# A hybrid DiT layer: sums of squares by tile pairs, modulation per tile, and the feed-forward's first two blocks by token halves

## The chip, the cores and the metric

One core of a Trainium2 chip runs the whole layer in one launch. The metric is device time in microseconds, from the start to the end of the program; the median of several runs counts. The engines are named as in the profile: PE (TensorE), DVE (VectorE), ACT (ScalarE), POOL (GpSimd) and SP (the queue that issues nearly all transfers).

## The reference, cut to what matters

One layer with 1024 latent tokens and 256 context tokens, width 1024, feed-forward width 2816, everything in fp32:

```python
mod_x = silu(c) @ w_ada + b_ada          # six vectors: sh1, sc1, g1, sh2, sc2, g2
mod_c = silu(c_ctx) @ w_ada + b_ada      # the same map for the context
px = modulate(rms_norm(x, norm1_w), sh1, sc1) @ w_in
pc = modulate(rms_norm(ctx, norm1_w), csh1, csc1) @ w_in
# gated DeltaNet on four heads, neighbourhood attention on eight heads
x = x + g1 * (concat(dn_x, na_x) @ w_out)
x = x + g2 * swiglu(modulate(rms_norm(x, norm2_w), sh2, sc2), w_ffn_in, w_ffn_out)
# modulate(h, shift, scale) = h * (1 + scale) + shift;  swiglu: (silu(gate) * up) @ w_out
```

## The kernel before, in words

The channels lie on the partitions: x is eight tiles `xt[k]` of 128 channels by 1280 tokens (256 context tokens, then 1024 latent ones). An fp32 product is made of three faster ones: each operand is cast to a rounded high part (`hh`, `whi`, `uhi`, `hB`, `hT`) and the rest is its low part (`hl`, `wlo`, `ulo`, `lB`, `lT`); PE adds high by high, high by low and low by high in PSUM. Most of the order is laid out by a list scheduler from the order in the source, and each engine then works strictly in that order; buffers come from pools, and a tile that takes over a place waits for the readers of the one before.

**The head (lines 617 to 715).** SP loads the eight x tiles, the constants, two modulation weight tiles, the raw weights of the first two projection blocks (`fraw`) and six more modulation tiles (`wada`, 1 MB each). ACT squares the tiles, DVE adds seven of them into one tile `acc`. PE multiplies `acc` and the last square by a matrix of ones (line 687), so that every partition holds each token's sum; ACT makes the reciprocal root `rs` from it with Ln and Exp (689, 690), for which it loads function tables. The first modulation (shift and scale) comes in four steps `ada(q)`, each for two channel tiles: 16 products of two `wada` tiles with the silu of both condition vectors, spread over four column groups (662); ACT copies the result to `arow` (665); four small products with a selector `sel` turn it into columns and sum the four groups (668); DVE adds the bias and makes scale times norm weight (`mod1`, `w1s`, lines 671 and 674). `sel` is reduced from the identity matrix by DVE (683). Tile by tile, DVE scales (701), ACT adds the shift and casts to `hh` (702), DVE makes `hl` (704), and PE multiplies the tile into the first two blocks, two key heads (`b.mm([k])`, line 397), six banks of PSUM for 1280 tokens each. The modulation step for the next two tiles stands behind the products of tiles 0, 1 and 2. ACT casts the two blocks' weights and DVE makes their low parts (`prefetch`, 193 and 194). The third block's weights take the buffers of the first block's, so their cast (193) waits for its last product.

**The middle.** The other projection blocks, the chunked scans in two directions, the attention, and the output projection, which the change does not touch.

**The feed-forward's start (lines 1360 to 1530).** The output projection ends with the residual stream `x2` in two halves of 512 tokens. For each half `normed(t)` sums the squares on PE (1373) and makes `rs`; `quadrant("Bij")` scales, shifts and splits four channel tiles (i: channel half, j: token half; 1461, 1462, 1454, 1455). B12 lies in the tiles that the profile calls `hT` and `lT`, which later hold the sum T4. The first two of 22 feed-forward blocks (`PLAIN`) are made plainly: for each of the blocks f, for each token half t, two products of 24 matmuls over the channel halves (1279), then Silu and a product on DVE. The order is f 0: first half, second half; f 1: first half, second half. `normed(1)` stands behind the first product. The weight pieces come from `Stream`: `load` fetches them, `make` casts and splits them into one of six buffers each (`uhi`, `ulo`; 1340, 1341), and `ahead(n)` makes them until n are in hand. The remaining 20 blocks go in pairs by a seven-product scheme of Strassen's kind, whose sums of the operand (`sums`, T1 to T4) DVE makes step by step beside the plain blocks. A `Background` called `late` makes the last part of the modulation beside these, with a step behind every second product.

Of the kernel before, what the change touches and what calls it, by code (L numbers as in the profile page):

```python
# [9 lines left out]
F32 = mybir.dt.float32  # L10
# [4 lines left out]
OP = mybir.AluOpType  # L15
# [39 lines left out]
PACE = 0.72  # L55
ORDER = [list(range(NCH)), [1, 0] + list(range(9, 1, -1))]
# [31 lines left out]
def hybrid(ctx, tc, a, dbg):  # L88
# [20 lines left out]
    bias = lasting("bias", [128, 2])  # L109
# [10 lines left out]
    act.dma_start(prm, a["prm"])  # L120
    cst = const("cst", [128, NCONST])
# [61 lines left out]
    def weights(wp, raws=2):  # L183
        def load(src, kt=KT, n=128, lo_engine=pool, raw=None):
# [8 lines left out]
            act.copy(h, r)  # L193
# [175 lines left out]
    with ExitStack() as bs:  # L369
# [30 lines left out]
        class Block:  # L400
# [7 lines left out]
            def prefetch(self, raw=None, lo_engine=pool):  # L408
# [3 lines left out]
                self.w = load_w(src, lo_engine=lo_engine, raw=raw)  # L412
# [207 lines left out]
        with ExitStack() as xs:  # L620
# [15 lines left out]
            sp.dma_start(cst, a["cst"])  # L636
            raws = [xp.tile([128, KT, 128], F32, name=f"fraw{i}", tag=f"fraw{i}") for i in range(2)]
            for j in range(2):
                load_ada(j)
            for i in range(2):  # L640
                sp.dma_start(raws[i], a["w_conv"][4 + i])
            for j in range(2, 8):
                load_ada(j)
            sp.dma_start(cw, a["cw"])
            sp.dma_start(masks, a["masks"])
# [6 lines left out]
            sel = xp.tile([128, 2], F32, name="sel", tag="sel")  # L652
            rs = xp.tile([128, T], F32, name="rs", tag="rs")
            acc = xp.tile([128, T], F32, name="acc", tag="acc")

            def ada(q):

                p = bank("pm")
                for j in (2 * q, 2 * q + 1):
                    w = aw.pop(j)  # L660
                    for k in range(4):
                        pe.matmul(p[32 * k:32 * k + 32], wide[:, 4 * (j % 2) + k], w[:, k], start=j % 2 == 0,
                                  stop=j % 2 == 1)
                row = xp.tile([128, 512], F32, name="arow", tag="arow", bufs=2)
                act.copy(row, p)
                p = bank("pm")
                for b in range(4):
                    pe.matmul(p[:, 2 * b:2 * b + 2], row[:, b * 128:(b + 1) * 128], sel, start=True, stop=True)
                k = slice(2 * q, 2 * q + 2)
                m = mod1.rearrange("p (s b) c -> p s b c", s=2)[:, :, k]  # L670
                dve.tensor_tensor(m, p[:, 0:8].rearrange("p (s b c) -> p s b c", s=2, c=2),
                                  bada[:, 0:16].rearrange("p (s b c) -> p s b c", s=2, c=1)[:, :, k].to_broadcast(
                                      [128, 2, 2, 2]), OP.add)
                dve.scalar_tensor_tensor(w1s[:, k], m[:, 1], 1.0,
                                         n1w[:, k].rearrange("p (b c) -> p b c", c=1).to_broadcast([128, 2, 2]),
                                         op0=OP.add, op1=OP.mult)

            for k in range(KT):
                sq = xp.tile([128, T], F32, name="sq", tag="sq", bufs=2)
                act.activation(sq if k else acc, xt[k], AF.Square)  # L680
                if 0 < k < KT - 1:
                    dve.tensor_tensor(acc, acc, sq, OP.add)
            dve.tensor_reduce(sel, ident.rearrange("p (c i) -> p i c", i=32)[:, 0:2], AX.X, OP.add)
            sums = [bank() for _ in SEGS]
            for i, x in enumerate((acc, sq)):
                for p, (s0, n) in zip(sums, SEGS):
                    pe.matmul(p[:, :n], M[C_ONE], x[:, s0:s0 + n], start=i == 0, stop=i == 1)
            for p, (s0, n) in zip(sums, SEGS):
                act.activation(rs[:, s0:s0 + n], p[:, :n], AF.Ln, bias=b_eps, scale=1.0 / D)
            act.activation(rs, rs, AF.Exp, scale=-0.5)  # L690
            ada(0)
            for b, raw in zip(first, raws):
                b.prefetch(raw, dve)
            for k in range(KT):
                if k == 4:
                    ascope.close()
                    h_tiles(pools(bs, "hp2", "right"), 4)
                t = xt[k]
                parts = [(j, x, mod1[:, k, j:j + 1]) for j, x in ((1, slice(0, CT)), (0, slice(CT, T)))]
                for j, x, sh in parts:  # L700
                    dve.scalar_tensor_tensor(t[:, x], t[:, x], w1s[:, k, j:j + 1], rs[:, x], op0=OP.mult, op1=OP.mult)
                    act.activation(hh[k][:, x], t[:, x], AF.Identity, bias=sh)  # L702
                for j, x, sh in parts:
                    dve.scalar_tensor_tensor(hl[k][:, x], t[:, x], sh, hh[k][:, x].bitcast(F32),
                                             op0=OP.add, op1=OP.subtract)
                for b in first:
                    b.mm([k])
                if k < 3:
                    ada(k + 1)
                if k == 5:  # L710
                    act.copy(mr[:, 4], ident)
                    for d in range(2):
# [990 lines left out]
```

## Time and profile before

| | |
|---|---|
| median of 3 runs | 1579.22 us (1577.59 to 1583.54) |
| the profiled execution's own time | 1576.81 us |
| its span in the trace | 1575.0 us |
| PE busy | 1476.1 us (94%) |
| DVE busy | 997.3 us (63%) |
| ACT busy | 719.8 us (46%) |
| POOL busy | 224.4 us (14%) |
| transfers | 271.02 MB |

Rows of a timeline give the start in us from the span's start, the duration, the engine, the line, the operation, output and inputs, shapes, how many instructions are merged, and in brackets how long the engine stood idle before and who ended it. A PE row counts each fp32 matmul as two instructions. Line numbers in the profile of before are those of the kernel before; from line 56 on the changed kernel's are higher by 1 to 26.

### The profile page before, as it was taken

What the parts mean: (1) busy time and instruction counts of PE and PEld (TensorE: products, weight loads), DVE (VectorE), ACT (ScalarE), POOL (GpSimd) and SP (SyncE); (2) the same over time, 40 slices, a digit from 0 to 9 for tenths busy, and PEclk for the clock granted to TensorE, in tenths of its full rate; (3) what the DMA queues carried; (4) which work ended last, traced back from release to release, by engine and by line L of the source; (5) the groups of instructions that cost most, each with busy time, mean ns of one, the idle gap of its engine ahead of it and who ended that gap; (6) DMA issues with size and microseconds to landing.
All of it is one profiled execution on the core that took longest, in us unless ns stands there. A gap on an engine that the chain in (4) does not pass through costs nothing. (4 is left out here: it accounts for less than half of the span.)

```text
span 1575.0 us, 23911 instructions
## 1 busy us (share of the span) xinstructions
PE 1476.1 (94%) x8626; PEld 1230.5 (78%) x8626; DVE 997.3 (63%) x1846; ACT 719.8 (46%) x1373; POOL 224.4 (14%) x278
## 2 busy tenths in 40 slices
PE   3999999999989887998899999999999999999999
PEld 2788787679887766787688878888888888888887
DVE  4675496674253644678887459865555556689652
ACT  5442553563343544665664256333333333444441
POOL 0045501632353600111100000000000000000000
PEclk8999999999999998999999999999999999999999
DMA  9164221576445449999845711533322224698742
GB/s 388 59 198 140 67 75 65 184 226 215 130 157 189 164 134 295 258 285 283 255 135 188 240 40 59 198 112 113 111 105 101 101 101 135 224 376 291 251 152 83
DMA packets 206406, 271.02 MB, mean 172 GB/s; under 512 B 15952, under 2 KB 115792, under 8 KB 205264
## 3 DMA queue, kind: packets, MB, share of 16 engines
q1 hardware_dynamic: 200816, 264.73, 51.2%
q10 hardware_dynamic: 5472, 4.76, 0.9%
q8 instruction: 68, 1.11, 0.3%
q14 instruction: 50, 0.41, 0.1%
HBM read 204.68 MB, written 68.94 MB: 174 GB/s over the span
## 5 line engine op out<-in xcount | busy, mean ns | idle before, releaser
L397 PE MATMUL blk<-hh,whi 128*128 128x512 f32 (+1 forms) x416 | 125.1, 395 | 4.2 <-ACT hh L702 2.8
L1340 ACT CAST uhi<-ws 128x512 fp32r<-128x512 f32 x91 | 54.8, 623 | 151.5 <-PE ps L1279 77.1
L1340 ACT CAST uhi<-wq 128x512 fp32r<-128x512 f32 x101 | 60.3, 621 | 136.8 <-issue 61.3
L397 PE MATMUL blk<-hh,wlo 128*128 128x512 f32 (+1 forms) x416 | 119.5, 381 | 0.6 <-POOL wlo L194 0.6
L397 PE MATMUL blk<-hl,whi 128*128 128x512 f32 (+1 forms) x416 | 118.9, 379 | 0.0
L1341 DVE TENSOR_TENSOR ulo<-wq,uhi 128x512 fp32r<-128x512 f32 x101 | 67.3, 688 | 65.9 <-ACT uhi L1340 36.5
L1279 PE MATMUL ps<-hT,uhi 128*128 128x512 f32 x336 | 104.3, 392 | 3.1 <-ACT hT L1454 3.1
L1279 PE MATMUL ps<-lT,uhi 128*128 128x512 f32 x336 | 103.6, 390 | 0.0
L1279 PE MATMUL ps<-hT,ulo 128*128 128x512 f32 x336 | 103.4, 389 | 0.0
L1279 PE MATMUL ps<-hB,uhi 128*128 128x512 f32 x288 | 89.7, 392 | 0.0
L1279 PE MATMUL ps<-lB,uhi 128*128 128x512 f32 x288 | 89.2, 391 | 0.0
L1279 PE MATMUL ps<-hB,ulo 128*128 128x512 f32 x288 | 88.8, 389 | 0.0
L397 PEld LDWEIGHTS blk<-hh,whi 128*128 128x128 f32 x416 | 71.0, 194 | 20.8 <-issue 4.9
L397 PEld LDWEIGHTS blk<-hh,wlo 128*128 128x128 f32 x416 | 74.6, 195 | 15.8 <-POOL wlo L194 0.9
L397 PEld LDWEIGHTS blk<-hl,whi 128*128 128x128 f32 x416 | 74.2, 194 | 15.8 <-issue 1.7
L1341 DVE TENSOR_TENSOR ulo<-ws,uhi 128x512 fp32r<-128x512 f32 x91 | 60.9, 687 | 37.6 <-ACT uhi L1340 29.3
L580 PE MATMUL blk<-zhi,hh 128*128 128x256 f32 (+1 forms) x288 | 84.5, 293 | 0.0
L580 PE MATMUL blk<-zhi,hl 128*128 128x256 f32 (+1 forms) x288 | 82.9, 288 | 0.0
L580 PE MATMUL blk<-zlo,hh 128*128 128x256 f32 (+1 forms) x288 | 81.6, 283 | 0.0
L1279 PEld LDWEIGHTS ps<-hT,uhi 128*128 128x128 f32 x336 | 63.1, 189 | 16.5 <-ACT hT L1454 3.5
L194 POOL TENSOR_TENSOR wlo<-wraw,whi 128x1024 fp32r<-128x1024 f32 x18 | 45.0, 2501 | 202.7 <-ACT whi L193 189.1
L1279 PEld LDWEIGHTS ps<-lT,uhi 128*128 128x128 f32 x336 | 63.3, 189 | 13.3
(353 smaller groups left out, 3626.2 us busy)
## 6 DMA issues: line engine op xcount, KB each, us to landing
wq<-w_fo SPq DMA_DIRECT2D x99, 256.0 KB, 5.0
wq<-w_gu SPq DMA_DIRECT2D x88, 256.0 KB, 3.0
wad<-wa SPq DMA_DIRECT2D x64, 256.0 KB, 3.6
bt<-rpb SPq DMA_DIRECT2D x64, 192.0 KB, 4.5
t_d<-g SPq DMA_DIRECT2D x22, 512.0 KB, 4.1
fr<-t_d SPq DMA_DIRECT2D x44, 256.0 KB, 4.6
f_d<-g SPq DMA_DIRECT2D x33, 256.0 KB, 2.1
fr<-f_d SPq DMA_DIRECT2D x33, 256.0 KB, 3.6
```

What stands on the lines that cost most here:

```text
L194: lo_engine.tensor_tensor(o, r, h.bitcast(F32), OP.subtract)
L397: pe.matmul(o, ww[:, k], xx[k][:, s], start=k == 0 and j == 0, stop=k == KT - 1 and j == 2)
L580: pe.matmul(p[:, :c1 - c0], x[k][:, s], ww[:, k, c0:c1], start=k == 0 and j == 0, stop=k == KT - 1 and j == 2)
L1279: pe.matmul(o, w[wi][:, k], x[xi][:, k], start=first and k == 0 and j == 0, stop=k == n - 1 and j == 2, skip_group_check=True)
L1340: act.copy(hi, self.raw[key])
L1341: dve.tensor_tensor(lo, self.raw[key], hi.bitcast(F32), OP.subtract)
```

## The change

Four things are changed together.

1. *Sums of squares by pairs.* ACT squares two tiles, DVE adds them, and PE sums the pair at once, four sets of three products in place of two sets at the end. The last pair is done in the three token segments.
2. *Modulation a tile at a time.* The host lays the modulation weights out as eight tiles of one channel tile each, all 1024 inputs in one transfer. `ada(j)` does the products and the copy, `column(j)` the selector products and DVE's part. The selector comes from the host into two new columns of the `bias` tile, which grows from two to eight, on ACT's queue. The whole head is put in a written order for PE, DVE and ACT; a table `AHEAD` says behind which products the later modulation steps stand. The first tile's products run with both high parts of the weights first, then low, and its normalisation by segments. The weights of the first block are cast and split by DVE, those of the second by POOL. SP loads the raw weights ahead of the modulation tiles, and the constants and masks behind the third of these.
3. *Feed-forward's first blocks by token halves.* The loops over f and t change places: both blocks' first halves, then both second halves. `normed(1)` stands behind the second product; the quadrants of the second half stand with block 1's first half. Eight buffers in place of six for `uhi` and `ulo`, and other numbers in `ahead`.
4. *The last background modulation* takes its steps from the third pair of blocks on.

```diff
+AHEAD = {(1, 0): (3,), (1, 1): (3, 4), (2, 0): (4, 5), (2, 1): (5, 6, 7), (3, 0): (6, 7)}
...
-    bias = lasting("bias", [128, 2])
+    bias = lasting("bias", [128, 8])
...
+    sel = bias[:, 4:6]
+    act.dma_start(sel, a["sel"])
...
-            act.copy(h, r)
+            if hi_engine:
+                hi_engine.tensor_copy(h, r)
+            else:
+                act.copy(h, r)
...
             def load_ada(j):
-                aw[j] = w = wap.tile([128, 4, 512], F32, name="wada", tag="wada")
-                sp.dma_start(w, a["wa1"][j // 2, :, 4 * (j % 2):4 * (j % 2) + 4])
+                aw[j] = w = wap.tile([128, KT, 256], F32, name="wada", tag="wada")
+                sp.dma_start(w, a["wa1"][j])
...
+            def ada(j, copy):
+                p, w = bank("pm"), aw.pop(j)
+                for k in range(KT):
+                    s = slice(32 * (k % 4), 32 * (k % 4) + 32)
+                    pe.matmul(p[s, :256], wide[:, k], w[:, k], start=k < 4, stop=k >= 4)
+                rows[j] = xp.tile([128, 256], F32, name="arow", tag="arow", bufs=2)
+                copy(rows[j], p[:, :256])
+            def column(j):
+                p, row = bank("pm"), rows.pop(j)
+                for b in range(2):
+                    pe.matmul(p[:, 2 * b:2 * b + 2], row[:, b * 128:(b + 1) * 128], sel, start=True, stop=True)
...
+            with tc.manual_schedule(engines={mybir.EngineType.PE, mybir.EngineType.DVE, mybir.EngineType.Activation}):
...
+                for k in range(0, KT, 2):
+                    sq = [xp.tile([128, T], F32, name="sq%d" % i, tag="sq%d" % i, bufs=2 + i) for i in range(2)]
+                    act.activation(sq[0], xt[k], AF.Square)
+                    for s in segs if k == KT - 2 else [slice(0, T)]:
+                        act.activation(sq[1][:, s], xt[k + 1][:, s], AF.Square)
+                        dve.tensor_tensor(sq[1][:, s], sq[0][:, s], sq[1][:, s], OP.add)
+                    for p, s in zip(sums, segs):
+                        pe.matmul(p[:, :s.stop - s.start], M[C_ONE], sq[1][:, s], start=k == 0, stop=k == KT - 2)
...
+                first[0].prefetch(raws[0], dve, dve)
+                first[1].prefetch(raws[1], pool, pool)
+                ada(0, dve.tensor_copy)
+                column(0)
+                normed_tile(0, segs)
+                ada(1, act.copy)
+                for b in first:
+                    b.banks()
+                for j, (w, x) in enumerate(((0, hh), (1, hh), (0, hl))):
+                    for b in first:
+                        for o, s in b.outs:
+                            pe.matmul(o, b.w[w][:, 0], x[0][:, s], start=j == 0, stop=False)
+                        if j == 0 and b is first[1]:
+                            column(1)
+                            normed_tile(1)
+                ada(2, act.copy)
+                column(2)
+                for k in range(1, KT):
...
+                    if k + 1 < KT:
+                        normed_tile(k + 1)
+                    for j, b in enumerate(first):
+                        b.mm([k])
+                        for q in AHEAD.get((k, j), ()):
+                            if q in rows:
+                                column(q)
+                            else:
+                                ada(q, act.copy)
...
-            hi = uw.tile([128, 4, 128], F32R, name="uhi", tag="uhi", bufs=6)
-            lo = uw.tile([128, 4, 128], F32R, name="ulo", tag="ulo", bufs=6)
+            hi = uw.tile([128, 4, 128], F32R, name="uhi", tag="uhi", bufs=8)
+            lo = uw.tile([128, 4, 128], F32R, name="ulo", tag="ulo", bufs=8)
...
-        for f in range(PLAIN):
-            po = [[bank(), bank()] for _ in range(2)]
-            g = prev[f]
-            w = [up.next(), None]
-            for t in range(2):
...
+        w = {}
+        for t in range(2):
+            for f in range(PLAIN):
+                g, po = prev[f], [bank(), bank()]
                 for i in range(2):
...
+                    if t == 0:
+                        if f == 1:
+                            quadrant(f"B{i + 1}2")
+                        w[f, i] = up.next()
+                    product(po, w[f, i], X[f"B{i + 1}{t + 1}"], i == 0)
+                    if t:
                         for _ in range(4):
                             next(todo, 0)
-                        up.ahead(4)
+                        up.ahead(4 * f + 2 * i)
+                    elif (f, i) == (0, 0):
+                        up.ahead(2)
+                    elif (f, i) == (0, 1):
+                        normed(1)
...
-                elif n % 2:
+                elif n % 2 and f >= PLAIN + 4:
                     late.step()
...
+    o["sel"] = c((np.arange(128)[:, None] % 32 == np.arange(2)).astype(np.float32))
```

More of the change, by code (lines that the diff above doesn't have):

```diff
@@ L183, in weights, with load @@
     def weights(wp, raws=2):
-        def load(src, kt=KT, n=128, lo_engine=pool, raw=None):
+        def load(src, kt=KT, n=128, lo_engine=pool, raw=None, hi_engine=None):
             given = raw is not None
@@ L406, in __init__, with prefetch @@
                 self.t0 = self.segs[0][0]
-            def prefetch(self, raw=None, lo_engine=pool):
+            def prefetch(self, raw=None, lo_engine=pool, hi_engine=None):
                 i = self.i
@@ L651, in hybrid @@
             pool.tensor_copy(wide[:, :, 0:2], sc2)
-            sel = xp.tile([128, 2], F32, name="sel", tag="sel")
             rs = xp.tile([128, T], F32, name="rs", tag="rs")
[L654 to L697, printed above, removed]
+            rows = {}
+            def ada(j, copy):
[5 more added lines that the diff above has]
+                copy(rows[j], p[:, :256])
@@ L698, in hybrid, with normed_tile @@
+            def normed_tile(k, cuts=(slice(0, CT), slice(CT, T))):
                 t = xt[k]
-                parts = [(j, x, mod1[:, k, j:j + 1]) for j, x in ((1, slice(0, CT)), (0, slice(CT, T)))]
-                for j, x, sh in parts:
+                parts = [(x, mod1[:, k, int(x.start < CT):int(x.start < CT) + 1]) for x in cuts]
+                for x, sh in parts:
+                    j = int(x.start < CT)
                     dve.scalar_tensor_tensor(t[:, x], t[:, x], w1s[:, k, j:j + 1], rs[:, x], op0=OP.mult, op1=OP.mult)
```

57 lines of the change are left out of this document (28 added, 29 removed).

## The prediction

> **What bounds the kernel now.** I read the page first (busy shares, slices, chain), then the timelines of 0 to 75 us engine by engine, the granted clock by stage, the waits, and the timelines of 924 to 980 us.
>
> ```profile
> span 1575.0 us, 23911 instructions
> PE   3999999999989887998899999999999999999999
> 944.68 246.52 PE ps L1279 x1080
> 1361.75 209.45 PE ps L1622 x924
> ```
>
> TensorE is full in nearly every slice, and from 944.68 us the chain of waits is only its products. Time can come only from places where PE stands still. The first slice (39 us) has three tenths; the change touches it, and the start of the feed-forward at 924 us. I take the two one after the other; between them the compiled order and waits of all engines are almost the same in both programs.
>
> **The head as it is.** ACT's Squares of the sixth and the last x tile, the sums on PE, the reciprocal root on ACT, the modulation, the first product, and the end of the first block's eighth tile:
>
> ```profile
> 13.40 1.27 ACT L680 ACTIVATE sq<-xt 128x1280 f32<-128x1280 f32 x1 [0.30 <-DMA xt<-xcT]
> 16.55 1.27 ACT L680 ACTIVATE sq<-xt 128x1280 f32<-128x1280 f32 x1 [0.29 <-DMA xt<-xcT]
> 17.89 4.63 PE L687 MATMUL m<-acc,ones 128*128 128x256 f32 x6 [17.89 <-DVE acc L682]
> 22.31 2.53 PE L687 MATMUL m<-sq,ones 128*128 128x256 f32 x6
> 24.77 1.93 PE L662 MATMUL pm<-wada,wide 128*32 128x512 f32 x16
> 24.88 0.69 ACT L689 ACTIVATE rs<-m,bias 128x512 f32<-128x512 f32 x1 [0.17 <-PE m L687]
> 25.47 1.03 ACT L193 CAST whi<-fraw 128x1024 fp32r<-128x1024 f32 x1
> 26.52 1.28 ACT L690 ACT_TABLE_LOAD   x1
> 27.81 1.27 ACT L690 ACTIVATE rs<-rs 128x1280 f32<-128x1280 f32 x1
> 28.99 0.57 ACT L665 COPY arow<-pm 128x512 f32<-128x512 f32 x1
> 29.61 1.86 PE L668 MATMUL pm<-sel,arow 128*128 128x2 f32 x8 [2.91 <-ACT arow L665]
> 31.51 0.17 DVE L671 TENSOR_TENSOR mod<-pm,prm 128x8 f32<-128x8 f32 x1 [3.75 <-PE pm L668]
> 31.71 0.16 DVE L674 SCALAR_TENSOR_TENSOR w1s<-mod,prm 128x4 f32<-128x4 f32 x1
> 32.50 0.51 ACT L702 ACTIVATE hh<-xt,mod 128x256 fp32r<-128x256 f32 x1 [2.00 <-DVE xt L701]
> 33.06 0.58 PE L397 MATMUL blk<-hh,whi 128*128 128x256 f32 x1 [1.59 <-ACT hh L702]
> 73.13 1.05 ACT L193 CAST whi<-wraw 128x1024 fp32r<-128x1024 f32 x1 [4.82 <-PE blk L397]
> ```
>
> It is one serial chain. The sums cannot start before DVE has added all tiles, and their first set takes 4.4 us, the second (same size) 2.5. The modulation row then queues on ACT behind a weight cast and the Exp. At 73.13 ACT casts the third block's weights, released by the first block's last product: my marker for the head's end, as all later work hangs on it.
>
> **The head after.** *Sums.* PE now sums each pair as DVE finishes it.
>
> ```profile
> 8.29 3.10 DVE L682 TENSOR_TENSOR acc<-acc,sq 128x1280 f32<-128x1280 f32 x2 [7.28 <-ACT sq L680]
> wada<-wa SPq DMA_DIRECT2D x8, 1024.0 KB, 13.7
> GB/s 0 110 394 411 420 420 427 410 413 413 423 436 426 410 404 423 429 421 421 431 415 421 426 421 421 384 292 165 0 0 11 0 0 0 0 0 0 0 0 0
> ```
>
> The first add ends at 8.29 + 1.55 = 9.85. PE starts there; the first pair takes 4.4 (slow, as above), to 14.3, the second 2.5, to 16.8. The third pair's add (Square ends 14.7) is done at 16.2, so it runs to 19.2. The last tile's Square starts at 16.55 as before and is cut in three, its last add ends about 18.7, and the fourth set ends at 21.7 at the latest. Before: 24.8. Then Ln 0.69, table load 1.28, Exp 1.27, no cast between: rs at 25.0 against 29.1. The six full adds become four; the casts of the first two blocks leave ACT.
>
> *Modulation.* Transfers go in order at some 420 GB/s (slices of 1.5 us). The eighth x tile lands at 16.5, then 0.52 MB each of raw weights (17.8, 19.0), then 1.05 MB per modulation tile: 21.5, 24.0, 26.5; constants and masks, which moved behind these three and are first read at the sixth tile, 27.9; then 30.4 to 40.4. PE's half-size modulation product (half of 1.93) runs 21.7 to 22.7. DVE, free again by 21.5 after casting and splitting the first block's weights (about 1.2 each, bounded by ACT's 1.03 cast), copies the row (0.4), PE's two selector products take half of 1.0, DVE's two small operations 0.33: 24.0, so rs at 25.0 is last. The selector costs nothing on this path: its transfer is issued on ACT's queue at the very start. DVE's first part (0.48) and ACT's (0.51) follow: first product at 26.05 against 33.06, **-7.0**. A wait is added: PE's second modulation product stands ahead of the first product and needs the tile of 24.0; it is done at 25.0, before ACT's.
>
> *First two blocks.* Warm, a set of three products over 1280 columns comes every 0.587 us:
>
> ```profile
> 68.24 0.75 PE L397 MATMUL blk<-hh,whi 128*128 128x256 f32 x3
> 68.83 0.75 PE L397 MATMUL blk<-hl,whi 128*128 128x256 f32 x3
> 44.52 1.01 PE L668 MATMUL pm<-sel,arow 128*128 128x2 f32 x8
> 28.00:30.00 2.00, 0.39 (x2) 0.39 (x3) 0.00 (x0) 2.00 (x3) 0.00 (x0) 0.89 1.02 426
> 30.00:32.00 2.00, 1.47 (x7) 1.39 (x7) 0.35 (x3) 0.50 (x1) 0.00 (x0) 0.50 0.99 414
> 40.00:42.00 2.00, 2.00 (x12) 1.38 (x16) 0.48 (x1) 0.00 (x0) 0.00 (x0) 1.00 0.81 197
> ```
>
> To the first block's end there are 45 sets, 26.4 us. Left to do among them after: six half modulation products, 5.8, and seven columns, 3.5; sum 35.7. I add 0.9 once, after the first tile: the next column waits for a row copy queued on ACT behind the second tile's 1024-wide activation. 36.6 against 73.13 - 33.06 = 40.07: **-3.5**. DVE needs 3.6 us a tile, PE 3.5 plus 1.4 while modulation lasts, so DVE keeps ahead. What goes is that the old order stalled for the second row and ran at granted clock 0.50 from about 30 to 40 us (PEclk, third number from the right in the windows above), after PE's pause of 2.91 us. My bounds: 0 (no gain in this part) and -4.9 (all stalls gone); the low end is nearer if the clock falls again, see below. The Trainium skill's page "TensorE: Matmul & The Clock Gate" (Part 1) says the clock halves after an idle window of about 3.4 us and comes back after one of activity. The trace agrees: 0.50 follows the near-idle stretch 26.7 to 29.6. By that rule the new order, whose pauses are about 1 us each, keeps the full clock.
>
> *POOL.* It now casts and splits the second block's first weights, with a reload of its code library between (the compiled order shows it; no row does).
>
> ```profile
> 74.26 2.40 POOL L194 TENSOR_TENSOR wlo<-wraw,whi 128x1024 fp32r<-128x1024 f32 x1 [68.25 <-ACT whi L193]
> ```
>
> Raw lands at 19.0; a cast of at most 2.4 and the split of 2.40 give 23.8 plus the reload. PE needs that split at about 26.05 + 6 x 0.24 + 0.5 + 0.6 = 28.6. The cover is 4.8 us. The reload's price lies between 0 and the 68.25 us of idle in which it vanished; I take under 4.8, by the row after it, which shows a normal 2.40. DVE and POOL sharing a port would cost at most one POOL operation, 2.4.
>
> **The feed-forward's start.**
>
> ```profile
> 928.60 0.61 PE L1279 MATMUL ps<-hB,uhi 128*128 128x512 f32 x2
> 935.00 1.10 PE L1373 MATMUL ps<-acc,ones 128*128 128x512 f32 x2 [0.80 <-DVE acc L1389]
> 944.68 1.22 PE L1279 MATMUL ps<-hT,uhi 128*128 128x512 f32 x2 [3.11 <-ACT hT L1454]
> 973.45 0.62 PE L1279 MATMUL ps<-hB,uhi 128*128 128x512 f32 x2
> 978.88 0.62 PE L1279 MATMUL ps<-hB,uhi 128*128 128x512 f32 x2
> 935.55 1.39 ACT L1462 ACTIVATE x<-x,modp 128x512 f32<-128x512 f32 x2 [2.10 <-DVE x L1461]
> 936.85 1.12 ACT L1454 CAST hB<-x 128x512 fp32r<-128x512 f32 x2
> 937.99 1.28 ACT L1374 ACT_TABLE_LOAD   x1
> 937.91 1.29 DVE L1455 TENSOR_TENSOR lB<-x,hB 128x512 fp32r<-128x512 f32 x2
> 950.00:980.00 30.00, 30.00 (x134) 24.84 (x133) 28.81 (x48) 19.09 (x34) 0.00 (x0) 1.00 0.08 27
> ```
>
> One of the eight products takes 978.88 - 973.45 = 5.43; eight take 43.4, but 928.60 to 978.88 is 50.3. Of the 6.9 over, the sum's product itself is about 1.3; 5.6 is waiting and slow restart: PE reached the sum before DVE had finished adding, then waited for the second half's tiles, of which the sum is the root. After, both blocks' first halves (four products, 21.7 us) come before any second-half tile is needed, and the sum stands after two of them. What is late next: the B21 product would start at 934.03 and want its third tile at 937.2, but ACT's cast gives it at 937.4 and DVE's low part at 938.6: 1.4 lost, and order on both engines is unchanged there. So 5.6 - 1.4 = **-4.2**. The sum then runs at 940.9; Silu with a table load, which ACT now does ahead of Ln, ends 941.6; the old chain from the table load at 937.99 to the product at 944.68 (6.7) puts the first tile at 948.3, and PE wants it at 953.0. Per tile ACT then needs 0.7 + 0.56 us and PE 5.43 / 4 = 1.36. The two more weight buffers let all eight pieces be split earlier, where ACT and DVE idle. The later modulation steps lie beside a full PE: nothing. Bounds -1.9 (a second stall like B21's after the sum) to -5.6.
>
> **Sum.** -7.0 - 3.5 - 4.2 = -14.7 from the profiled run's own 1576.81 (span 1575.0 and 1.81 around): 1562.1. The median shown lies 2.4 higher, so I put the median at 1563.5. Own range of this case 1559.5 to 1570.
>
> **Rivals.** *The clock falls in the head's pauses* (22.7 to 26.0): ten microseconds at half rate, as at 30 to 40 us before, or POOL's and DVE's operations excluding each other: 3 to 5 us back, 1567 to 1569. Against: no pause reaches the 2.9 us that preceded 0.50. *DVE bounds the feed-forward's start*: it is busy 28.81 of the 30 us from 950 to 980, so PE's holes may only move to the Strassen sums: 1567.7. Against: those sums have four products' time, as before. *The head's gain is given back*: something of the next stage does not move with PE, a transfer or the background modulation: only 4.2 remains, 1574 to 1575, no change. Against: transfers end at 42 us. *Slower:* POOL's library reload, now between cast and split, is long. Each microsecond over 4.8 stops PE, since the second block's low-weight product stands in order ahead of everything. From 4.8 + 14.7 = 19.5 us of reload the kernel is slower than before; at 35 it takes 1594. For it: only that no row bounds it under 68 us; against: 4.8 us of cover and 2.40 in the row after. The Trainium skill's page "GPSIMD Engine Reference" (2.1 Instruction dispatch) states about 6 us for the first call to freshly loaded code; no row here shows it, and by that figure, an estimate, the split would come 1.2 us late, some 1564.7.
>
> **Numbers.** The forecast 0.65, clock or port 0.13, DVE-bound 0.07, given back 0.08, reload 0.07. 0.5% is 7.9 us, about what a measurement can tell from no change. Faster: 0.65 + 0.07 + 0.10 of the clock case = 0.82; same: 0.03 + 0.08 = 0.11; slower 0.07. The range leaves out the reload case and the far end of the others: 1558 to 1575.
>
> **Signs.** Right: PE's first sum near 10 us, first product near 26, the third block's cast near 62.7, no PE hole at the feed-forward's start but about 1.4 us in B21, and its first Strassen product about 4 us sooner after 928.6's counterpart. Wrong: PE waiting for POOL's split in the second block, granted clock 0.50 after 26 us, or a head marker above 66.

## The result and the profile after

The changed kernel takes 1568.91 us (median of 5 runs, 1565.91 to 1570.46); the kernel before, run beside it, 1578.68 (1577.02 to 1583.54). The ratio is 0.9931, with a 95% interval from 0.991 to 0.9951: 9.8 us less. The forecast was 1563.5, with 1558 to 1575 as its range. The profiled execution took 1568.91 us, against 1576.81 for that of before: 7.9 less where the forecast had 14.7.

The page of after, span and PE's slices. The first slice has gone from three tenths to six; of the others only the 13th and 14th differ, by one tenth each:

```profile
span 1566.9 us, 24037 instructions
PE   6999999999988987998899999999999999999999
```

The head, from the timelines of PE, ACT and POOL of after:

```profile
9.95 10.98 PE L702 MATMUL m<-sq,ones 128*128 128x256 f32 x24 [9.95 <-DVE sq L700]
22.96 1.27 ACT L705 ACTIVATE rs<-rs 128x1280 f32<-128x1280 f32 x1
24.23 1.93 PE L666 MATMUL pm<-wada,wide 128*32 128x256 f32 x16 [0.19 <-DMA wada<-wa]
26.10 3.00 PE L717 MATMUL blk<-hh,whi 128*128 128x256 f32 x6
20.59 3.23 POOL L200 TENSOR_TENSOR wlo<-fraw,whi 128x1024 fp32r<-128x1024 f32 x1
65.51 1.05 ACT L199 CAST whi<-wraw 128x1024 fp32r<-128x1024 f32 x1 [2.04 <-PE blk L403]
```

The first block product stands at 26.10 (before 33.06): 7.0 forward, as forecast. But the marker, ACT's cast of the third block's weights, is at 65.51 (before 73.13) and not at 62.6. Between the two lie 39.4 us; the forecast had 36.6, and the kernel before 40.1. The windows of after show the larger part of the reason (third number from the right: granted clock):

```profile
24.00:26.00 2.00, 1.81 (x17) 0.59 (x16) 1.78 (x5) 0.95 (x3) 0.00 (x0) 0.54 0.96 396
26.00:28.00 2.00, 2.00 (x8) 1.25 (x5) 2.00 (x4) 1.44 (x3) 0.00 (x0) 0.50 1.06 428
30.00:32.00 2.00, 2.00 (x9) 1.68 (x9) 1.97 (x4) 0.55 (x2) 0.00 (x0) 0.76 1.00 418
```

PE is full from 26 us on, but at half rate until 31. Then the feed-forward's start: first product, the product on B21 with its stall, the sum behind it, the first product on `hT` (timeline), and the two long stretches of the chain of waits:

```profile
924.78 0.61 PE L1305 MATMUL ps<-hB,uhi 128*128 128x512 f32 x2
930.22 0.61 PE L1305 MATMUL ps<-hB,uhi 128*128 128x512 f32 x2
933.67 0.73 PE L1305 MATMUL ps<-hB,uhi 128*128 128x512 f32 x2 [0.58 <-ACT hB L1480]
934.82 0.74 PE L1305 MATMUL ps<-lB,uhi 128*128 128x512 f32 x2 [0.41 <-DVE lB L1481]
937.22 1.02 PE L1399 MATMUL ps<-acc,ones 128*128 128x512 f32 x2
948.97 0.62 PE L1305 MATMUL ps<-hT,uhi 128*128 128x512 f32 x2
938.24 320.97 PE ps L1305 x1416
1353.60 209.45 PE ps L1646 x924
```

The wait of 3.11 us for `hT` has gone, two short ones in B21 have come. From the first product on `hB` to the down-projection are 428.8 us (before 433.15): 4.3 less. The first product on `hB`, though, comes only 3.8 us sooner than before (928.60). So the account of the two profiles is: head -7.6, middle +3.8, feed-forward -4.3, together -8.1. Two things are missing against the forecast: 2.8 us in the head and 3.8 in the middle.

### The profile page after: what moved, and what is told of

It reads as the page before. It is cut to its first block, busy times and chain, and to the rows that moved or that the text cites. A ratio compares the mean times of both kernels' runs of the same rounds, so it can differ in the third digit from the quotient of the medians.

```text
span 1566.9 us, 24037 instructions
## 1 busy us (share of the span) xinstructions
PE 1480.1 (94%) x8702; PEld 1234.1 (79%) x8702; DVE 997.3 (64%) x1856; ACT 720.3 (46%) x1378; POOL 233.3 (15%) x280
## 3 DMA queue, kind: packets, MB, share of 16 engines
q1 hardware_dynamic: 200816, 264.73, 51.2%
## 5 line engine op out<-in xcount | busy, mean ns | idle before, releaser
L403 PEld LDWEIGHTS blk<-hh,wlo 128*128 128x128 f32 x410 | 72.9, 194 | 15.4 <-POOL wlo L200 0.9
L1305 PEld LDWEIGHTS ps<-hT,ulo 128*128 128x128 f32 x336 | 63.1, 188 | 13.2
```

The source lines that it names most:

```text
L403: pe.matmul(o, ww[:, k], xx[k][:, s], start=k == 0 and j == 0, stop=k == KT - 1 and j == 2)
L1305: pe.matmul(o, w[wi][:, k], x[xi][:, k], start=first and k == 0 and j == 0, stop=k == n - 1 and j == 2, skip_group_check=True)
```

## The experiments

**The two halves of the change, alone, and the kernel after once more.** `ff_only` is the kernel before with the diff's feed-forward parts, `head_only` the kernel after without them, `again` the kernel after unchanged.

> The kernel before with the feed-forward's part of the change alone (blocks by token halves, eight weight buffers, the new numbers of weights ahead, the late steps from the fifth scaled block on); its head is the old one. Theory A (the two parts stand each for itself, and what the middle stage loses is not made by either): the stretch from the first product on hB to the first product of the down-projection takes 428.8 us as in the kernel after (433.2 in the kernel before), so 4.3 less, and the whole 1574.4. Theory B (the feed-forward's part gains only because the head's part moved work in time): the stretch stays above 431. The first product on hB stands where the kernel before has it, 928.6, if one execution of the middle is like another; if executions differ there by themselves, it comes out up to 3 us away from that.

> The kernel after with the feed-forward's part undone. The head ends (cast of the third block's weights on ACT) at 65.5 as in the kernel after, 7.6 before the kernel before. Theory A (the 3.8 us that the middle gave back are where PE's pauses happen to fall in the clock's windows of 3.41 us, and so change from execution to execution): the first product on hB comes at 921 to 925, not at the same place as in the kernel after, and the whole is near 1578.7 - 6 = 1572.7, between 1571 and 1575. Theory B (the middle gives the head's gain back by waits that the earlier start makes): the first product on hB is again at 924.8 with the same waits, and the whole is 1574.9. Theory C (the middle costs nothing at all, all of it was scatter): 921.0 and 1571.1.

> The kernel after once more, unchanged, for a second profiled execution beside the first. If executions differ by where the clock's windows fall (theory A), the first block product, the half-rate stretch and the first product on hB (924.8 in the first profile) move by up to 3 us against the first profile, and the set of places where the clock falls is not the same. If the middle's loss belongs to the change (theory B), the first product on hB is within 0.5 us of 924.8 and the clock falls at the same instructions.

Measured: `ff_only` 0.9971 of before (0.9958 to 0.9983), `head_only` 0.9984 (0.9968 to 1.0), `again` 0.9945 (0.9927 to 0.9964), medians 1575.4, 1575.2 and 1569.5 where before had 1579.0. Rows of `ff_only` (first product on `hB`, chain):

```profile
933.03 0.62 PE L1279 MATMUL ps<-hB,uhi 128*128 128x512 f32 x2
946.51 320.97 PE ps L1279 x1416
1361.87 209.45 PE ps L1620 x924
```

Its feed-forward stretch is 428.8, as in the kernel after: theory A, the two parts stand each for itself. But its first `hB` is at 933.0, not at 928.6. PE's order in the middle is that of before, the other engines' too until 787 us behind the cast of the third block's weights, and 4.35 of the 4.4 us had come by 720: an execution of the middle may differ by 4 us from another. In `ff_only` the middle ran at half rate for 54.6 us in all, in before for 47.8, which can be a part of it. The head and the middle of `head_only` with the start of its down-projection, and then the head and the middle of `again`:

```profile
65.50 1.05 ACT L199 CAST whi<-wraw 128x1024 fp32r<-128x1024 f32 x1 [2.04 <-PE blk L403]
925.62 0.61 PE L1305 MATMUL ps<-hB,uhi 128*128 128x512 f32 x2
1357.39 209.45 PE ps L1648 x924
```

```profile
64.01 1.05 ACT L199 CAST whi<-wraw 128x1024 fp32r<-128x1024 f32 x1 [2.05 <-PE blk L403]
925.51 0.62 PE L1305 MATMUL ps<-hB,uhi 128*128 128x512 f32 x2
24.00:28.00 4.00, 3.81 (x22) 1.92 (x22) 3.76 (x8) 2.40 (x5) 0.00 (x0) 0.57 1.02 416
```

In `again` the half rate lasts only from 24.3 to 27.7, and the marker is 1.5 us earlier than in the first profile of the same kernel. The middle (cast to first `hB`) takes 859.3, 861.5 and 860.1 us in after, `again` and `head_only`. `head_only` came out above all three theories for it (1575.2; theory B had 1574.9); its interval leaves room for a gain of 0 to 5 us.

**The old kernel once more**, for its middle and its feed-forward:

> The kernel before, unchanged, for one more profile with the old head. From the cast of the third block's weights to the first product on hB the two profiles with the old head took 855.5 and 859.9 us, the four with the new one 859.3, 861.5, 860.1 and 860.5. Theory A (the middle with the new head is longer by what the seam costs, 1.4 us of a wait on DVE some 25 us behind the cast, and all the rest is scatter between executions): this one takes 856 to 860 us, and its first 100 us behind the cast agree with the first profile within 0.4 us. Theory B (no difference at all but scatter): its first 100 us behind the cast vary like those of the others, by 1 us or more.

```profile
72.47 1.05 ACT L193 CAST whi<-wraw 128x1024 fp32r<-128x1024 f32 x1 [4.84 <-PE blk L397]
928.99 0.62 PE L1279 MATMUL ps<-hB,uhi 128*128 128x512 f32 x2
1360.78 209.45 PE ps L1622 x924
```

Its middle takes 856.5, and its first 100 us behind the cast agree with the first profile to 0.3 us. Its feed-forward stretch takes 431.8, 1.35 less than in the first profile, with the same wait for `hT`. The windows from 944 to 948 of before and of `old_again` tell the difference:

```profile
944.00:948.00 4.00, 3.32 (x8) 2.67 (x9) 4.00 (x8) 3.97 (x7) 0.00 (x0) 0.57 0.00 0
```

```profile
944.00:948.00 4.00, 2.93 (x13) 2.40 (x14) 4.00 (x7) 3.97 (x7) 0.00 (x0) 1.00 0.00 0
```

The profile of before had a fall of the clock there, `old_again` had none, nor `head_only` (431.8 too). So the feed-forward's change is worth 3.0 us, and 4.3 only against an execution with that fall, one of three with the old order. `ff_only`'s runs (4.6 us less, 2.7 to 6.6) agree with both.

**The clock in the head.** `warm` puts four small products, overwritten afterwards, between the sums and the first modulation product:

```diff
                 p, w = bank("pm"), aw.pop(j)
+                for i in range(4 if j == 0 else 0):
+                    pe.matmul(p[:, :128], M[C_ONE], sq[1][:, 768 + 128 * i:896 + 128 * i], start=True, stop=True)
```

> The kernel after with four more products on PE (ones by 128 columns of the squares, overwritten by what follows in the same bank) between the sums and the first modulation product, where PE stands 0.91 us waiting for a DMA. Theory A (the half rate from 24.1 to 31.0 us comes from the window of 3.41 us before it, in which PE was busy only about half of the time; it is what made the stretch from the first block product to the end of the eighth tile 39.3 us instead of the forecast 36.6): the granted clock stays at 1.00 through the head, the cast of the third block's weights comes at 62.7 to 63.3 instead of 65.5, and the whole is 2 to 3 us shorter than the kernel after, about 1566.4. Theory B (the stretch is bound by DVE's and ACT's turns of 4.1 us a tile, the clock hides behind them): the clock stays full but the cast comes at 65 or later, no gain. Theory C (the fall has nothing to do with PE's pauses): the clock falls as before.

```profile
65.89 1.05 ACT L199 CAST whi<-wraw 128x1024 fp32r<-128x1024 f32 x1 [2.05 <-PE blk L403]
24.00:28.00 4.00, 2.77 (x23) 1.52 (x24) 3.24 (x8) 2.97 (x5) 0.36 (x1) 1.00 1.02 413
28.00:32.00 4.00, 4.00 (x17) 3.38 (x17) 3.15 (x7) 1.10 (x2) 0.00 (x0) 0.64 1.02 425
```

None of the three: the rate holds where it fell before and falls later, from 29.1 to 32.5, behind the pauses in which PE waits for ACT's segments. `head_only`, without these products, has its fall in nearly the same place (28.9 to 32.3). 0.9946 of before (0.9928 to 0.9965), as the kernel after. `warm_order` closes those pauses too, and takes the first tile's products of both blocks segment by segment:

```diff
+            def idle(p, n):
+                for i in range(n):
+                    pe.matmul(p[:, :128], M[C_ONE], sq[1][:, 768 + 128 * i:896 + 128 * i], start=True, stop=True)
...
+                idle(first[0].outs[0][0], 2)
                 for j, (w, x) in enumerate(((0, hh), (1, hh), (0, hl))):
-                    for b in first:
-                        for o, s in b.outs:
+                    for n in range(len(SEGS)):
+                        for b in first:
+                            o, s = b.outs[n]
+                            if n and not j and b is first[0]:
+                                idle(o, 1)
                             pe.matmul(o, b.w[w][:, 0], x[0][:, s], start=j == 0, stop=False)
```

> The kernel after with the first tile's products of both blocks taken segment by segment (so that PE has two products for each segment that ACT delivers) and eight small products on PE in its pauses before the first block products (two before the first modulation product, one before its columns, two before the first block product, one for each later segment and the column). Theory A (the half rate in the head comes from windows in which PE is busy 0.52 to 0.70 of the time, two thirds of it with products that fill only a part of the array): the clock stays at 1.00 until 250 us, the first block product stays at 25.9 to 26.3, and the cast of the third block's weights comes at 62.3 to 63.0 instead of 64.0 and 65.5 in the two profiles of the kernel after. Theory B (DVE and ACT with 4.1 us a tile bound the stretch): the clock stays full and the cast comes at 64 or later. Theory C: the clock falls in the head nevertheless. The whole is 1.5 to 3 us below the kernel after by theory A, not to be told from it by B.

```profile
25.65 0.50 PE L729 MATMUL blk<-hh,whi 128*128 128x256 f32 x2
24.00:28.00 4.00, 3.66 (x34) 2.72 (x34) 3.83 (x8) 2.34 (x5) 0.00 (x0) 1.00 1.03 418
28.00:32.00 4.00, 3.70 (x31) 2.43 (x30) 2.89 (x7) 1.89 (x3) 0.00 (x0) 1.00 1.02 420
62.65 0.73 PE L403 MATMUL blk<-hl,whi 128*128 128x512 f32 x2 [0.32 <-DVE hl L697]
63.41 1.05 ACT L199 CAST whi<-wraw 128x1024 fp32r<-128x1024 f32 x1 [2.04 <-PE blk L403]
```

The clock is full until 252 us (and until 165 us in `both`, below, which has the same head), and the marker comes at 63.41, 2.1 us before that of after, 0.6 before that of `again`. That is theory A on the clock, though 0.4 us later than it said; of B, only the last tile's low part (0.32) shows. The median is 1568.1, the ratio 0.9935 (0.9922 to 0.9949): not to be told from the kernel after.

**Which parts of the head bring its gain.** `old_sums` takes the sums of before, all else as after:

```diff
-                for k in range(0, KT, 2):
-                    ...
+                for k in range(KT):
+                    sq = xp.tile([128, T], F32, name="sq", tag="sq", bufs=2)
+                    act.activation(sq if k else acc, xt[k], AF.Square)
+                    if 0 < k < KT - 1:
+                        dve.tensor_tensor(acc, acc, sq, OP.add)
+                for i, x in enumerate((acc, sq)):
+                    for p, s in zip(sums, segs):
+                        pe.matmul(p[:, :s.stop - s.start], M[C_ONE], x[:, s], start=i == 0, stop=i == 1)
```

> The kernel after with the sums of squares as before: DVE adds seven tiles into one, PE sums that and the last square in two sets at the end. It prices the first term of the forecast by itself. Theory A (the sums bring the root 4.1 us forward and the first product with it, and nothing else of the chain is later than the root): the sums end near 24.7 instead of 20.9 to 21.4, the first block product comes at 29.5 to 30.0 instead of 25.9 to 26.1, and the whole is 3.5 to 4.5 us above the kernel after. Theory B (the modulation for the first tile, freed from its queue behind the cast and the Exp, is what brings the first product forward, the sums give the rest at best): the first block product comes at 27.5 or earlier. The clock: with PE idle until 18 us and pauses behind the sums a half-rate stretch is expected in the head too; if it is longer than in the kernel after, up to 2 us more.

```profile
29.05 0.58 PE L718 MATMUL blk<-hh,whi 128*128 128x256 f32 x1 [1.26 <-ACT hh L687]
```

The first block product is at 29.05: of the 7.0 us the sums bring 3.0 and the other edits 4.0. That lies nearer to theory A's 29.5 than to B's 27.5. The ratio is 0.9976 (0.996 to 0.9992), which is 5 to 7 us above the two measurements of the kernel after, where A said 3.5 to 4.5; the half-rate stretch (29.0 to 35.8) is two windows long, as in after.

`split_back` takes the second block's first weights from POOL again:

```diff
-                first[1].prefetch(raws[1], pool, pool)
+                first[1].prefetch(raws[1], dve)
```

> The kernel after with the second block's first weights rounded by ACT and split by DVE as in the kernel before, instead of both on POOL. In the kernel after POOL takes 1.24 and 3.23 us for them beside DVE's split of the first block, which takes 1.94 us instead of 1.22. Theory A (the two engines slow each other where they work side by side, and neither is on the path): DVE's first split takes 1.2 us again, its second follows for 1.2 us more, the first modulation row is copied about 0.5 us later than at 22.96, the first block product comes at 26.1 to 26.8, and the whole moves by less than 1 us. Theory B (POOL's part is what brings the first product forward): the first block product comes 1.2 us later or more, at 27.3.

Rows of `split_back`, and below them the two of after on which DVE and POOL work side by side:

```profile
20.30 1.23 DVE L200 TENSOR_TENSOR wlo<-fraw,whi 128x1024 fp32r<-128x1024 f32 x1
25.89 1.23 DVE L200 TENSOR_TENSOR wlo<-fraw,whi 128x1024 fp32r<-128x1024 f32 x1 [4.37 <-ACT whi L199]
27.51 1.01 PE L674 MATMUL pm<-bias,arow 128*128 128x2 f32 x4 [3.95 <-DVE arow L668]
30.32 3.18 PE L717 MATMUL blk<-hh,whi 128*128 128x256 f32 x6
```

```profile
19.65 1.94 DVE L200 TENSOR_TENSOR wlo<-fraw,whi 128x1024 fp32r<-128x1024 f32 x1
19.27 1.24 POOL L197 CAST whi<-fraw 128x1024 fp32r<-128x1024 f32 x1 [13.15 <-DMA fraw<-w_conv]
```

Theory B, and by more than it said: the cast stands behind the Exp on ACT, DVE waits 4.37 us for it with the modulation row queued behind, and the first product is 4.2 us later. The whole takes 0.9979 of before (0.9964 to 0.9994), 1574.7. This prices the cast at that place on ACT; a place ahead of the Exp was not run. Theory A was right on the side effect alone: beside POOL the split takes 1.94 us, alone 1.23.

**What the middle gives back at once.** A point some 41 us behind the marker, ACT's cast of the sixth block's weights, stands 40.76 behind it in before, 40.80 in `old_again`, 42.21 in after and 42.2 to 42.3 in `again`, `head_only`, `warm` and `warm_order`: 1.45 us later with each new head. In all of them DVE waits 5.0 to 5.3 us for a piece of the second modulation's weights (`wad`) with taps of the convolution queued behind; with the old head it does not wait there. The expectations below speak of points 42 to 45 us behind the marker; all are read here at this cast. The casts of before and after, and DVE's wait in after:

```profile
113.89 1.05 ACT L193 CAST whi<-wraw 128x1024 fp32r<-128x1024 f32 x1 [2.72 <-DMA wraw<-w_nqk]
```

```profile
107.72 1.05 ACT L199 CAST whi<-wraw 128x1024 fp32r<-128x1024 f32 x1 [2.40 <-DMA wraw<-w_nqk]
91.00 1.41 DVE L234 SCALAR_TENSOR_TENSOR acc<-wad,sc,acc 128x512 f32<-128x512 f32 x1 [5.29 <-DMA wad<-wa]
```

Here the compiled order differs, which the prediction took to be almost the same behind the head. In before DVE does three of these multiplications ahead of the marker, from 69.52 us on, and SP has issued six of the loads by 72 us. In after the first multiplication stands at 67.88, 2.4 us behind the marker, and SP issues the fifth load only at 84.76, 19.3 us behind it. SP's rows, of before and of after:

```profile
61.05 10.88 SPq L207 DMA_DIRECT2D wad<-wa  x6
```

```profile
60.41 1.30 SPq L213 DMA_DIRECT2D wad<-wa  x3
69.70 0.60 SPq L213 DMA_DIRECT2D wad<-wa  x1
84.76 2.88 SPq L213 DMA_DIRECT2D wad<-wa  x3
```

`seam_queue` issues these loads from POOL's queue (`queue.dma_start` with `queue=pool` for `sp.dma_start`):

> The kernel after with the loads of the second modulation's weights in the middle stage (wad) issued from POOL's queue instead of SP's, where each stands behind stores that wait for their data. In the kernel after DVE stands 5.3 us for the fifth of them (91.00) with three taps of the convolution queued behind, and PE then waits 0.7 us for kk at 110.4. Theory A (this wait is the 1.4 us that the middle gives back at once): DVE's wait for wad before 110 us goes, a point 42 us behind the cast (the cast of the weights of the sixth block) comes 1.4 us earlier, and the whole is 1 to 2 us below the kernel after. Theory B (the delay is that of DVE's load of taps, which the earlier head does not shorten): DVE waits elsewhere, and the point does not move by more than 0.3 us.

A miss: DVE still waits for `wad` (4.9 us), and the kernel takes 1.0031 of before (1.0017 to 1.0045), 14 us above the kernel after. The loads wait on POOL for a buffer that DVE has not freed, and POOL's work for the scans, for which PE then waits, is queued behind; between 280 and 320 us PE goes from 2 to 13 us behind its times in after:

```profile
274.43 0.58 POOL L213 DMA_DIRECT2D wad<-wa  x1 [12.80 <-DVE acc L232]
285.92 0.80 PE L949 MATMUL pr<-rg,mr 128*128 128x512 f32 x1 [3.19 <-POOL rg L939]
303.71 1.06 PE L979 MATMUL pr<-y,kk 128*32 128x64 f32 x8 [4.23 <-DVE y L981]
```

`seam_order` holds the multiplications back until the first block's taps are done; `both` adds this to `warm_order`; `seam_again` is `seam_order` once more.

```diff
-                x, sc = landing.pop(0), sc2[:, k, 0:1]
+                x, sc = landing.pop(0), (col[:, k:k + 1] if col is not None else sc2[:, k, 0:1])
...
-        bg2.add(modulation(adp, range(4), bank, 3, 1))
+        bg2.add(modulation(adp, range(4), bank, 3, 1, w2s))
...
         first[1].silu()
+        dve.scalar_tensor_tensor(w2s, first[0].acc[:, T - 8:T], 0.0, sc2[:, :, 0], op0=OP.mult, op1=OP.add)
```

> The kernel after with one more small operation on DVE behind the second block's activation, which copies the column of silu(c) that the second modulation's weights (wad) are multiplied by and takes it only when the first block's taps are done; so the scheduler sets three of these multiplications between the second block's taps and the next ones behind the third block's, as the kernel before has them, and none waits for a transfer in front of taps. Theory A (the fifth wad, waited for 5.1 to 5.3 us in each profile with the new head and in none with the old, is what the middle gives back at once): no wait for wad on DVE in the 40 us behind the cast of the third block's weights, a point 44.7 us behind that cast comes at 0.0 to 0.4 and not at 1.4 us after the place that it has with the old head, PE's wait for kk (0.7) goes, and the whole is 1 to 1.5 us below the kernel after, if the later middle is like that of the others. Theory B (the delay stays whatever DVE's order is): still 1.4.

> The kernel after with both edits: the first tile's products segment by segment with small products in PE's pauses (warm_order), and the wad multiplications behind the first block's taps (seam_order). If both theories hold, the clock is 1.00 through the head, the cast of the third block's weights comes at 63.4 as in warm_order, the point 44.7 us behind it is not late, and the whole is 2 to 3 us below the kernel after, near 1566.5 where before has 1579. If only the clock holds: as warm_order, 1568.1.

> The kernel of seam_order once more, for a second profile. In both kernels with the edit DVE's wait for wad had gone from 5.1 to 0.2 us, but 42.6 us behind the cast of the third block's weights the one (both) was 0.4 us and the other (seam_order) 1.9 us later than with the old head; in the latter the fourth block's weights took 5.1 us from issue to cast instead of 3.9 to 4.1, and PE waited 2.1 us for vt. Theory A (that transfer was slow in this one execution): here the weights take about 4 us, PE waits under 1 us for vt, and the point is 0.3 to 0.8 late. Theory B (with the edit, the earlier or later end of the head decides): 1.9 again, as its head ends as late.

Rows of `both`:

```profile
89.70 1.51 DVE L234 SCALAR_TENSOR_TENSOR acc<-wad,w2s,acc 128x512 f32<-128x512 f32 x1 [0.22 <-DMA wad<-wa]
104.65 1.05 ACT L199 CAST whi<-wraw 128x1024 fp32r<-128x1024 f32 x1 [1.29 <-DMA wraw<-w_nqk]
```

DVE's wait has gone in all three (0.2 us); one of 2.8 us for a later piece of `wad` has come, 42 to 43 us behind the marker, after the cast that is read here. In `both` the cast is 41.18 behind the marker, 0.4 late. But in `seam_order` it is 42.66, 1.9 late, and in `seam_again` 42.26, 1.5 late: there PE waits 2.1 and 1.6 us for `vt`, and the fourth block's weights take 5.1 and 5.0 us from issue to cast, against 3.9 in `both`. The ratios are 0.9952 (0.993 to 0.9973) and 0.9938 (0.9914 to 0.9961), as the kernel after. So the wait for `wad` is not the whole of the 1.45 us; take it away, and in two profiles of three ACT's wait for the fourth block's weights brings the delay back. What makes that transfer slow stays open.

No version was found that is measurably faster than the kernel after.

## Why the prediction was right, point by point

- *Sums, root, first product* (26.05): the chain is right, the exact hit is luck. PE's first sum starts at 9.95, the root ends at 24.2 (forecast 25.0), and the modulation, not the root, is last, by 0.3 us. The 0.8 us went to PE's second modulation product, which runs at half rate (1.93 us, about half of that at full rate) and ends only at 26.1; the forecast had it done before ACT's part. Where the clock holds there, the first product is at 25.86 (`head_only`) and 25.65 (`warm_order`).
- *POOL*: right that it stops nobody; the sum is right by luck. Its split ends at 23.8, as worked out, but out of a cast of 1.24 us (2.4 forecast) and a split of 3.23 (2.40). PE's low-weight products come at 29.6. Between cast and split lie 0.08 us, so a library reload of the length feared does not show.
- *First two blocks* (-3.5): failed; the profile shows -0.7. The step that failed is the one that kept the clock full because the new order's pauses are about 1 us each. The rate fell in all profiles of the head but those of `warm_order` and `both`, for one to three windows. One of the prediction's own signs of being wrong, a granted clock of 0.50 after 26 us, came. The rival gave 3 to 5 us back, and 2.8 were. At full clock the stretch takes 37.8 (`warm_order`, though its first tile is in another order), so about 1.6 us are the clock's, and 1.2 of the 36.6's error are not: small waits for ACT's segments and row copy and for the last low part. The forecast had its chance for clock or port at 0.13; that was too low.
- *Feed-forward* (-4.2): -4.3 between the two profiles, with no wait at `hT`, as worked out. The product on B21 takes 7.0 us to the start of the sum where 5.43 is full pace, so the stall costs 1.6 (forecast 1.4). From 938.24 us on the chain is PE's products alone, so DVE does not bound this part. Still a mis-sized term: 1.35 us of the 6.9 that the old order lost were a fall of the clock in the one execution that was read. The change itself is worth 3.0.
- *The middle* (0): mis-sized. The step that failed is the reading that the compiled orders are almost the same behind the head; at the seam DVE's and SP's are not. With the old head the middle took 855.5, 856.5 and 859.9 us, with the new one 859.3 to 861.5 in the six profiles without a seam edit, and 866.6 in `old_sums`. About 3 us are given back; 1.45 of them come in the first 45 us, in each of the six. The rest is of the size of the scatter. Part of the scatter goes with the clock: the three old middles ran at half rate for 47.8, 51.2 and 54.6 us, in that order, and that of `old_sums` for 64.9. It is not the whole, as `warm_order`, with 44.4, took 860.6. The runs were on several chips (the record names 3, 9 and 14), and none separates the chip from the execution; the cause of the rest stays open.
- *The whole*: over three profiles of each, -7.9 for the head (markers 72.9 and 65.0 in the mean), -3.0 for the feed-forward and +3.0 for the middle make -7.9; by the ratios the gain is 10.9 (7.7 to 14.2) and 8.7 us (5.7 to 11.5). The forecast's 14.7 were too many by what the clock and the middle took; that the time still fell within its range is owed to the range's width of 17 us as much as to the account.

## What to carry to other kernels

Add up the stages of a forecast against more than one execution: here the same order took up to 4 us more or less in the same stage, and a term read from one profile carried a fall of the clock that others did not have. Where a serial stretch is made shorter but keeps gaps of 0.5 to 1 us on TensorE, count how busy TensorE is in each 3.4 us, not how long one gap is, before the full rate is assumed behind it. And look at what runs in the background at the seam: when a stage starts 7 us earlier, the transfers that feed it need not move with it, and the compiled order of every engine has to be compared there.

## What the runs showed of the hardware

*The clock goes by how busy PE is in a fixed window.* Every change of the granted clock in the profiles lies on a grid of 3.41 us, whose place differs from execution to execution. I counted PE's busy time in each of these windows between 20 and 1555 us, in the twelve profiles without `seam_queue` and `seam_again`. Windows at full rate were followed by one at half rate in 72 of 72 cases with PE under 40% busy, 38 of 52 at 40 to 50%, 11 of 88 at 50 to 60%, 10 of 267 at 60 to 80% and 3 of 4697 above. Back to full rate came 0 of 50 under 70%, 8 of 27 at 70 to 90%, and 126 of 131 above. The Trainium skill's page "TensorE: Matmul & The Clock Gate" (Part 1) has this window, free-running, at 3413 ns, and the grid agrees; by its table the rate falls after an idle window, and here a window half busy was often enough. In `warm_order` and `both`, whose heads had no fall, no window from 18 to 45 us was under 0.83 busy. The falls in the whole new head came at 0.52 to 0.70 (`after`, `again`, `head_only`, `warm`, `seam_order`), those of the old head at 0.16 to 0.31; in the former much of PE's work was modulation products on a quarter of the array and products with two columns, which the count takes as whole. That these weigh less is a guess that no run tested.

*DVE and POOL side by side.* DVE's split took 1.94 us beside POOL's cast and 1.23 alone; POOL's split took 3.23 us beside DVE's and 2.40 alone. The Trainium skill's page "SBUF — State Buffer" (Who interferes with whom) says that a DVE instruction with two inputs in SBUF contends with a POOL instruction that reads SBUF, over a shared pair of ports that is an exclusive lock. The rows come near that: by such a lock, an estimate, DVE would wait from 19.65 for the end of POOL's cast at 20.51, 0.86 us, where 0.71 was lost.
